# Order of the high and low weight products inside a weight-stationary unit of a decoder layer

## The chip, the cores and the metric

The kernel runs on one core of one Trainium2 chip. The metric is the device time of one launch in microseconds (us). The median of three runs before the change is 1451.52 us (1451.15 to 1453.07).

## The reference

One decoder layer for 256 tokens of width 2048, all in float32. Cut to its large products:

```
h      = rmsnorm(x)
q_a,k_a,v_a,q_r,f_r,i_r,g_r,gate_a,gate_r = split(h @ w_in)       # 2048 -> 11264
o_a    = causal attention(q_a, k_a, v_a)                          # 8 heads of 128
o_r    = gated linear recurrence(q_r, f_r, i_r), normed, gated    # 8 heads of 128
y      = sigmoid(gate_a + b_a) * (o_a @ w_up_a) + sigmoid(gate_r + b_r) * (o_r @ w_up_r)
x      = x + y @ w_out
out    = x + relu(rmsnorm(x) @ w_mlp1)^2 @ w_mlp2                 # 2048 -> 8192 -> 2048
```

## The kernel before

Every float32 factor is cut into two float32r parts, a high one (the value rounded to float32r, made on ScalarE) and a low one (what is left, made on VectorE), and a product of two factors is the sum of three: high by high, high by low, low by high. Activations lie with the width on the partitions: a "cat" tile of 128 x 512 holds the high parts of 256 tokens in columns 0 to 255 and their low parts in columns 256 to 511. `xcat`, `x2cat`, `mcat`, `orc` and `oac` are such tiles; there are 16 for a width of 2048.

Weights come in units of 128 x 2048 (1 MB). `load` brings a unit into a tile `raw` by the SP queue, `cut` (L107 to L118) makes the tiles `hi` (L116, ScalarE) and `lo` (L117, VectorE) of it, and `unit` (L123) hands out one unit while it loads and cuts the one two places ahead. `raw`, `hi` and `lo` have three buffers each.

A **weight-stationary unit** is the function `ws` (L278): it makes 128 output columns for all 256 tokens from 16 pieces of `hi` and `lo`, each 128 x 128. For each piece TensorE loads the high piece as weights and streams the whole cat tile past it (512 columns, called a wide product here), and loads the low piece and streams the high half of the cat tile (256 columns, a narrow product). Both add into one PSUM bank `pw`: the wide one into all 512 columns, the narrow one into columns 256 to 511. `summed` (L296) then copies the second half out on ScalarE (L298, `cross`) and adds the first half on VectorE (L299). The order before is: wide 0, narrow 0, narrow 1, wide 1, narrow 2, wide 2, and so on to narrow 15, wide 15 (L282 to L287). So each unit holds one place where a wide product follows a wide one (its first, behind the last of the unit ahead), one where a narrow product follows a narrow one, and otherwise alternates.

There are 152 units of 16 pieces: 72 for projections (`project`, on `xcat`), 16 for `w_out` (on `mcat`) and 64 for `w_mlp1` (on `x2cat`). A unit of the up-projections is used in two halves of 8 pieces, one on `orc` and one on `oac`; there are 16 of each. The rest of TensorE's work is not touched: products with activations as weights (`pv` L266 to L268 at the start, `py` L653 to L655 for `w_mlp2`), which are all 512 columns wide, and the small products of the recurrence and the attention, which run as side work between the units (`step`).

The queue of each engine is put in order by a scheduler that models the engines; program order is only its input. Where a product waits for data that come late, it may put later products ahead.

Of the kernel before, what the change touches and what calls it, by code (L numbers as in the profile page):

```python
# [17 lines left out]
T = 256  # L18
# [12 lines left out]
def layer_kernel(ctx: ExitStack, tc: tile.TileContext, xT, vecs, wv, wm, wg, wu, wo, w1, w2, cf, cm, out):  # L31
    nc = tc.nc
# [21 lines left out]
    def bank(s, pool=pp):  # L54
        return pool.tile([P, 512], F32, tag="b", name=uid(s))
# [67 lines left out]
    def unit():  # L123
        u = done[0]
        done[0] += 1
        load(u + AHEAD)
        cut(u + AHEAD)
        return split.pop(u)
# [127 lines left out]
    for c in range(4):  # L256
        pst = [bank(f"pv{t}", pm) for t in range(2)]
# [20 lines left out]
    def ws(parts, pst=None):  # L278

        pst = pst if pst is not None else bank("pw", pm)  # L280
        n = len(parts)
        for i, (h, l, cat) in enumerate(parts):  # L282
            if i == 0:
                nc.tensor.matmul(pst, h, cat, start=True, stop=False)  # L284
            nc.tensor.matmul(pst[:, T:], l, cat[:, :T], start=False, stop=False)  # L285
            if i > 0:
                nc.tensor.matmul(pst, h, cat, start=False, stop=(i == n - 1))  # L287
        return pst

    def unit_parts(hi, lo, cats, off=0):  # L290
        return [
            (hi[:, off + k * P : off + (k + 1) * P], lo[:, off + k * P : off + (k + 1) * P], c)
            for k, c in enumerate(cats)
        ]
# [8 lines left out]
    def project(dst):  # L303
        pst = ws(unit_parts(*unit(), xcats))
        s = s1("s")
        summed(pst, s)
        nc.vector.tensor_mul(dst, s, rstd)
# [258 lines left out]
    for j in range(KD):  # L566
        gr = s1("gr")
        project(gr)
        sig = nc.scalar.activation(gr, gr, AF.Sigmoid, bias=b_gate[:, 1, j : j + 1])
        with tc.issue_after(sig.ins):  # L570
            nc.scalar.activation(ga[j], ga[j], AF.Sigmoid, bias=b_gate[:, 0, j : j + 1])
        hi, lo = unit()
        pr = ws(unit_parts(hi, lo, orc, 1024))
        pa = ws(unit_parts(hi, lo, oac, 0))
        r = s1("r")
        summed(pr, r)
        nc.vector.tensor_mul(r, r, gr)
        a = s1("a")
        summed(pa, a)
        nc.vector.tensor_mul(a, a, ga[j])  # L580
        nc.vector.tensor_add(a, a, r)
        if j % 2 == 0:
            mt = g4("mcat", (P, 2, 512), F32R)
        to_parts((mt[:, j % 2, :T], mt[:, j % 2, T:]), a)
        mcat.append(mt[:, j % 2, :])
# [9 lines left out]
    for j in range(KD):  # L595
        pst = ws(unit_parts(*unit(), mcat))
# [30 lines left out]
    for part in range(4):  # L627
        ucat = []
        for j in range(16):
            pst = ws(unit_parts(*unit(), x2cats))  # L630
# [13 lines left out]
        for b in range(4):  # L644
            pst = [bank(f"py{t}", pm) for t in range(2)]
# [105 lines left out]
```

## Time and profile before

| what | us | share of the span |
|---|---|---|
| median of three runs | 1451.52 | |
| the profiled execution's own time | 1452.54 | |
| its span, first to last instruction | 1450.8 | 100% |
| TensorE matmuls busy | 1444.1 | 100% |
| TensorE weight loads busy | 1240.4 | 85% |
| VectorE busy | 894.3 | 62% |
| ScalarE busy | 690.6 | 48% |

Weight loads run beside matmuls, so the two do not add. The recorded end of a matmul is modelled and overlaps the next one's start; the distance from one start to the next is what a product takes in a row of products, and it is called a slot below. Starts are printed to 0.01 us, so a slot is best read over several products.

### The profile page before, as it was taken

Reading aid. Unit: us, or ns where it says so; the run is one execution under the profiler, and the core shown is the slowest. Engines: PE = TensorE matmul, PEld = TensorE weight load, DVE = VectorE, ACT = ScalarE, POOL = GpSimd, SP = SyncE. Lnnn points to the kernel's source line nnn. Section 1 sums busy time; section 2 is a strip of 40 time slices with the busy share of each in tenths; the row PEclk is TensorE's granted clock in tenths of the full one; section 3 lists DMA queues with packets and bytes.
Section 4 is the critical chain, followed back from the end, with each engine's and each line's share of the span. In section 5 each row is a group of like instructions: output and inputs, shape, how many; then the busy total and the mean of one; then the engine's idle time right before and its main releaser. Section 6 shows DMA issues by size and latency. Waiting matters only on the chain.

```text
span 1450.8 us, 18651 instructions
## 1 busy us (share of the span) xinstructions
PE 1444.1 (100%) x7824; PEld 1240.4 (85%) x7824; DVE 894.3 (62%) x958; ACT 690.6 (48%) x786; POOL 4.4 (0%) x10
## 2 busy tenths in 40 slices
PE   9999999999999999999999999999999999999998
PEld 7888889888888888888888888888888888888887
DVE  7545776667877667676666644565455655556553
ACT  7444343565765454544455443454335443355431
POOL 0000000000000000000000000000000000000000
PEclk9999999999999999999999999999999999999999
DMA  9555443445454465555545565556555566655571
GB/s 333 204 183 194 149 167 121 150 170 177 172 175 150 171 214 192 208 199 189 189 175 197 180 201 188 191 177 200 187 192 196 180 190 188 202 179 193 183 224 63
DMA packets 66323, 268.07 MB, mean 185 GB/s; under 512 B 4768, under 2 KB 7072, under 8 KB 43456
## 3 DMA queue, kind: packets, MB, share of 16 engines
q1 hardware_dynamic: 64368, 263.70, 53.3%
q0 software_dynamic: 576, 2.10, 0.4%
q8 instruction: 61, 1.00, 0.3%
q10 hardware_dynamic: 1296, 1.09, 0.2%
q14 instruction: 22, 0.18, 0.0%
HBM read 264.78 MB, written 2.10 MB: 184 GB/s over the span
## 4 chain that ended last, share of the span: by engine, by line
PE 99%; DMA 0%; DVE 0%; ACT 0%; issue 0%; DVEq 0%
PE pw L287 40%; PE pw L285 22%; PE py L653 8%; PE py L654 8%; PE py L655 8%; PE pw L284 3%; PE pv L266 2%; PE pv L267 2%; PE pv L268 2%; PE pd L363 1%; PE pl L491 0%; DMA raw<-wv 0%; PE pt L622 0%; PE pd L341 0%; PE pd L371 0%; PE pb L435 0%
## 5 line engine op out<-in xcount | busy, mean ns | idle before, releaser
L117 DVE TENSOR_TENSOR lo<-raw,hi 128x2048 fp32r<-128x2048 f32 (+2 forms) x258 | 569.4, 2208 | 317.6 <-ACT hi L116 317.5
L116 ACT ACTIVATE hi<-raw 128x2048 fp32r<-128x2048 f32 (+2 forms) x258 | 475.4, 1844 | 282.8 <-PE py L655 197.1
L287 PE MATMUL pw<-xcat,hi 128*128 128x512 f32 x1080 | 383.5, 397 | 0.0
L287 PE MATMUL pw<-x2cat,hi 128*128 128x512 f32 x960 | 342.4, 399 | 0.0
L285 PE MATMUL pw<-xcat,lo 128*128 128x256 f32 x1152 | 311.3, 280 | 0.0
L285 PE MATMUL pw<-x2cat,lo 128*128 128x256 f32 x1024 | 277.2, 281 | 0.0
L298 ACT ACTIVATE cross<-pw 128x256 f32<-128x256 f32 x168 | 64.5, 384 | 422.9 <-PE pw L287 422.9
L287 PEld LDWEIGHTS pw<-xcat,hi 128*128 128x128 f32 x1080 | 202.8, 188 | 46.3
L285 PEld LDWEIGHTS pw<-xcat,lo 128*128 128x128 f32 x1152 | 217.5, 189 | 5.2
L287 PEld LDWEIGHTS pw<-x2cat,hi 128*128 128x128 f32 x960 | 180.4, 188 | 42.0
L653 PE MATMUL py<-hi,ucat 128*128 128x512 f32 x512 | 199.5, 390 | 0.0
L655 PE MATMUL py<-hi,ucat 128*128 128x512 f32 x512 | 199.2, 389 | 0.0
L654 PE MATMUL py<-lo,ucat 128*128 128x512 f32 x512 | 199.2, 389 | 0.0
L285 PEld LDWEIGHTS pw<-x2cat,lo 128*128 128x128 f32 x1024 | 193.5, 189 | 5.4
L655 PEld LDWEIGHTS py<-hi,ucat 128*128 128x128 f32 x512 | 96.1, 188 | 20.0
L654 PEld LDWEIGHTS py<-lo,ucat 128*128 128x128 f32 x512 | 96.1, 188 | 19.9
L653 PEld LDWEIGHTS py<-hi,ucat 128*128 128x128 f32 x512 | 96.1, 188 | 19.7
L287 PE MATMUL pw<-mcat,hi 128*128 128x512 f32 x240 | 85.6, 399 | 0.0
L299 DVE TENSOR_TENSOR s<-pw,cross 128x256 f32<-128x256 f32 x72 | 30.4, 422 | 76.7 <-ACT cross L298 76.7
L299 DVE TENSOR_TENSOR t<-pw,cross 128x256 f32<-128x256 f32 x64 | 27.2, 425 | 77.0 <-ACT cross L298 77.0
L285 PE MATMUL pw<-mcat,lo 128*128 128x256 f32 x256 | 69.3, 281 | 0.0
L287 PEld LDWEIGHTS pw<-mcat,hi 128*128 128x128 f32 x240 | 45.1, 188 | 10.5
(180 smaller groups left out, 1245.0 us busy)
## 6 DMA issues: line engine op xcount, KB each, us to landing
raw<-w SPq DMA_DIRECT2D x128, 1024.0 KB, 5.3
raw<-wm SPq DMA_DIRECT2D x56, 1024.0 KB, 4.8
raw<-wg SPq DMA_DIRECT2D x16, 1024.0 KB, 4.8
raw<-wu SPq DMA_DIRECT2D x16, 1024.0 KB, 4.9
raw<-wo SPq DMA_DIRECT2D x16, 1024.0 KB, 4.8
raw<-wv SPq DMA_DIRECT2D x10, 1024.0 KB, 4.9
raw<-wv SPq DMA_DIRECT2D x8, 512.0 KB, 6.7
raw<-wv SPq DMA_DIRECT2D x8, 256.0 KB, 5.5
```

Source lines behind the costliest of these rows:

```text
L116: nc.scalar.activation(hi[:, s], raw[:, s], AF.Copy)
L117: nc.vector.tensor_sub(lo[:, s], raw[:, s], hi[:, s].bitcast(F32))
L266: nc.tensor.matmul(pst[t], xh, hi[:, k, :], start=(kk == 0), stop=False)
L267: nc.tensor.matmul(pst[t], xh, lo[:, k, :], start=False, stop=False)
L284: nc.tensor.matmul(pst, h, cat, start=True, stop=False)
L285: nc.tensor.matmul(pst[:, T:], l, cat[:, :T], start=False, stop=False)
L287: nc.tensor.matmul(pst, h, cat, start=False, stop=(i == n - 1))
L298: nc.scalar.activation(c, pst[:, T:], AF.Copy)
L299: nc.vector.tensor_add(dst, pst[:, :T], c)
L653: nc.tensor.matmul(pst[t], uh, hi[:, k], start=(kk == 0), stop=False)
L654: nc.tensor.matmul(pst[t], uh, lo[:, k], start=False, stop=False)
L655: nc.tensor.matmul(pst[t], ul, hi[:, k], start=False, stop=(kk == 15))
```

## The change

`ws` issues all wide products of a unit first, then all narrow ones. The group's start flag stays on the first product and the stop flag moves to the last narrow one. Nothing is added or removed.

```diff
         for i, (h, l, cat) in enumerate(parts):
-            if i == 0:
-                nc.tensor.matmul(pst, h, cat, start=True, stop=False)
-            nc.tensor.matmul(pst[:, T:], l, cat[:, :T], start=False, stop=False)
-            if i > 0:
-                nc.tensor.matmul(pst, h, cat, start=False, stop=(i == n - 1))
+            nc.tensor.matmul(pst, h, cat, start=(i == 0), stop=False)
+        for i, (h, l, cat) in enumerate(parts):
+            nc.tensor.matmul(pst[:, T:], l, cat[:, :T], start=False, stop=(i == n - 1))
```

TensorE in a unit of `w_mlp1`, before. A row is line, operation, output bank and its inputs, columns; "128x512" is a wide product, "128x256" a narrow one.

```order
L284 MATMUL pw_9980<-x2cat,hi_9914 128x512
L285 MATMUL pw_9980<-x2cat,lo_9915 128x256 x2
L287 MATMUL pw_9980<-x2cat,hi_9914 128x512
L285 MATMUL pw_9980<-x2cat,lo_9915 128x256
L287 MATMUL pw_9980<-x2cat,hi_9914 128x512
```

The same unit and the next one after the change (lines are two lower behind the changed function, and L283 and L285 are its wide and its narrow product):

```order
L283 MATMUL pw_9980<-x2cat,hi_9914 128x512 x16
L285 MATMUL pw_9980<-x2cat,lo_9915 128x256 x16
L283 MATMUL pw_10029<-x2cat,hi_9944 128x512 x16
L285 MATMUL pw_10029<-x2cat,lo_9945 128x256 x16
```

The alternation has become two runs of 16. The same holds for all units but a few at the borders of stages.

TensorE at one such border, the first unit of `w_out` after the change, whose last piece needs the `mcat` tile that is made last (`mcat_5302`; `pw_5421` is this unit's bank, `pw_5465` that of the next unit):

```order
L283 MATMUL pw_5421<-mcat_5302,hi_5308 128x512
L283 MATMUL pw_5465<-mcat_3895,hi_5354 128x512 x2
L283 MATMUL pw_5465<-mcat_4096,hi_5354 128x512 x2
L283 MATMUL pw_5465<-mcat_4297,hi_5354 128x512 x2
L283 MATMUL pw_5465<-mcat_4498,hi_5354 128x512 x2
L283 MATMUL pw_5465<-mcat_4699,hi_5354 128x512 x2
L283 MATMUL pw_5421<-mcat_5302,hi_5308 128x512
```

The first of these rows is the fifteenth wide product of the unit and the last row its sixteenth; the scheduler has put ten wide products of the next unit between them. The first unit of `w_mlp1` has the same with four products of the next unit. Before the change both units were in one piece.

ScalarE at the border of up-projection and `w_out`, before (`pw_5375` is the bank of the last half unit on `oac`; `hi_5417` is the cut two units ahead):

```order
L298 ACTIVATE cross_5393<-pw_5358 128x256
L298 ACTIVATE cross_5398<-pw_5375 128x256
L116 ACTIVATE hi_5417<-raw_5415 128x2048
L311 ACTIVATE mcat_5302<-a_5397 128x256
L116 ACTIVATE hi_5461<-raw_5459 128x2048
```

And after the change:

```order
L116 ACTIVATE hi_5417<-raw_5415 128x2048
L296 ACTIVATE cross_5398<-pw_5375 128x256
L309 ACTIVATE mcat_5302<-a_5397 128x256
L116 ACTIVATE hi_5461<-raw_5459 128x2048
L116 ACTIVATE hi_5507<-raw_5505 128x2048
```

The cut of the high part has moved ahead of the copy that takes the finished bank out of PSUM; the buffer that it fills is now read for the last time by the sixteenth wide product, halfway through the unit's 32.

## Rows read from the trace of the kernel before

**Rows 1.** The page's busy times (share of the span) and instructions of each engine.

```profile
PE 1444.1 (100%) x7824; PEld 1240.4 (85%) x7824; DVE 894.3 (62%) x958; ACT 690.6 (48%) x786; POOL 4.4 (0%) x10
```

**Rows 2.** The page's chain that ended last: share of the span by engine.

```profile
PE 99%; DMA 0%; DVE 0%; ACT 0%; issue 0%; DVEq 0%
```

**Rows 3.** The page's granted clock of TensorE in 40 slices, tenths of full speed.

```profile
PEclk9999999999999999999999999999999999999999
```

**Rows 4.** TensorE's two waits: who waited for whom, us, times, longest.

```profile
PE pwarm L159 <- DVE warm L156: 1.5, 1, 1.5
PE pv L266 <- ACT xcat L195: 1.2, 1, 1.2
```

**Rows 5.** Timeline of TensorE, one unit of `w_mlp1`: start us, us, engine, line, operation.

```profile
800.76 0.39 PE L284 MATMUL pw<-x2cat,hi 128*128 128x512 f32 x1
800.99 0.40 PE L285 MATMUL pw<-x2cat,lo 128*128 128x256 f32 x2
801.22 0.40 PE L287 MATMUL pw<-x2cat,hi 128*128 128x512 f32 x1
801.45 0.28 PE L285 MATMUL pw<-x2cat,lo 128*128 128x256 f32 x1
801.57 0.40 PE L287 MATMUL pw<-x2cat,hi 128*128 128x512 f32 x1
801.81 0.28 PE L285 MATMUL pw<-x2cat,lo 128*128 128x256 f32 x1
...
806.17 0.40 PE L287 MATMUL pw<-x2cat,hi 128*128 128x512 f32 x1
806.41 0.39 PE L284 MATMUL pw<-x2cat,hi 128*128 128x512 f32 x1
806.63 0.40 PE L285 MATMUL pw<-x2cat,lo 128*128 128x256 f32 x2
806.87 0.40 PE L287 MATMUL pw<-x2cat,hi 128*128 128x512 f32 x1
807.10 0.28 PE L285 MATMUL pw<-x2cat,lo 128*128 128x256 f32 x1
```

**Rows 6.** Timeline of TensorE in the `w_mlp2` stage, wide products alone.

```profile
860.07 0.39 PE L653 MATMUL py<-hi,ucat 128*128 128x512 f32 x1
...
865.51 0.39 PE L653 MATMUL py<-hi,ucat 128*128 128x512 f32 x1
```

**Rows 7.** Timeline of TensorE, two half units of the up-projection and the unit behind.

```profile
546.70 0.39 PE L284 MATMUL pw<-orc,hi 128*128 128x512 f32 x1
546.93 0.40 PE L285 MATMUL pw<-orc,lo 128*128 128x256 f32 x2
...
547.39 0.28 PE L285 MATMUL pw<-orc,lo 128*128 128x256 f32 x1
...
549.51 0.40 PE L284 MATMUL pw<-oac,hi 128*128 128x512 f32 x1
549.75 0.39 PE L285 MATMUL pw<-oac,lo 128*128 128x256 f32 x2
...
550.21 0.28 PE L285 MATMUL pw<-oac,lo 128*128 128x256 f32 x1
...
552.29 0.39 PE L284 MATMUL pw<-xcat,hi 128*128 128x512 f32 x1
```

**Rows 8.** Timeline of TensorE's weight loads behind a level of the recurrence.

```profile
167.22 0.19 PEld L284 LDWEIGHTS pw<-xcat,hi 128*128 128x128 f32 x1
167.33 0.42 PEld L285 LDWEIGHTS pw<-xcat,lo 128*128 128x128 f32 x2
```

**Rows 9.** Timeline of TensorE at the same place, matmuls.

```profile
167.25 0.48 PE L284 MATMUL pw<-xcat,hi 128*128 128x512 f32 x1
167.56 0.40 PE L285 MATMUL pw<-xcat,lo 128*128 128x256 f32 x2
```

**Rows 10.** Timeline of TensorE: first product of `w_out`, first of `w_mlp1`.

```profile
642.21 0.39 PE L284 MATMUL pw<-mcat,hi 128*128 128x512 f32 x1
...
732.56 0.39 PE L284 MATMUL pw<-x2cat,hi 128*128 128x512 f32 x1
```

**Rows 11.** Timeline of VectorE at these two places: a cut, last `mcat`, last `x2cat`.

```profile
644.70 2.29 DVE L117 TENSOR_TENSOR lo<-raw,hi 128x2048 fp32r<-128x2048 f32 x1 [0.46 <-ACT hi L116]
646.90 0.42 DVE L312 TENSOR_TENSOR mcat<-a,mcat 128x256 fp32r<-128x256 f32 x1
...
736.97 0.48 DVE L601 SCALAR_TENSOR_TENSOR x2cat<-x,vt,x2cat 128x256 fp32r<-128x256 f32 x1
```

## The prediction, made before the run

> **What bounds the kernel now.** I read the page's busy times first: TensorE's matmuls cover the whole span, VectorE has 62% and ScalarE 48% [rows 1]. The chain of work that ended last is TensorE for 99% [rows 2], the clock is granted in full in every slice, that is 2.4 GHz [rows 3], and TensorE waited for others only 1.5 + 1.2 us, both at the start [rows 4]. So the time is the sum of TensorE's slots, and the question is whether a slot depends on what stands beside it. A busy share cannot say that, because records of matmuls overlap; the starts in the timeline can.
>
> I then read one unit start by start [rows 5]. From the unit's first product to the next unit's first is 806.41 - 800.76 = 5.65 us; over the 16 units of `w_out` it is (732.56 - 642.21) / 16 = 5.647 us [rows 10]. From wide 1 to wide 15 there are 14 pairs in 806.17 - 801.22 = 4.95 us: **0.3536 us for a pair**. Where wide products stand alone, as in the `w_mlp2` stage, 24 of them take 865.51 - 860.07 = 5.44 us: **0.2267 us for a wide slot** [rows 6]. The wide product that opens a unit, behind another wide one, shows the same 0.23 us (800.76 to 800.99). If a wide slot in a pair is also 0.2267, the narrow one has 0.3536 - 0.2267 = **0.127 us**. A narrow product streams half the columns, and half of 0.2267 is 0.1133. So each lone narrow slot is 0.0136 us longer than its columns explain, 14 times in each of the 152 units and 6 times in each half unit, about 2300 times.
>
> **What the 0.0136 us is.** My reading is the weight load. The load for a product can only run while the product ahead streams, and a wide one gives it 0.2267 us, a narrow one half. How long such a load takes is seen where it has little cover: behind the short products of the recurrence the load for wide 0 is issued at 167.22 and narrow 0 starts at 167.56 [rows 8, 9]; the wide product between them takes its 0.2267, so it truly began at 167.333, which is 0.113 us after its load was issued, though it is recorded at 167.25. The next load follows 0.11 us behind [rows 8]. So a load takes about what a narrow product's columns take, and any delay in it lengthens the narrow slot. That is a tie, and the change decides how often it is fought: as often as before. Every product still has its own load, and every load behind a narrow product is still covered by 0.1133 us of columns alone. What changes is what stands around it.
>
> The term that decides is therefore the narrow slot in a run of narrow ones, which the trace shows only in twos: narrow 0 and narrow 1 of every unit. Taking the wide 1 behind them at 0.2267 and reading on to narrow 2, the two slots take 801.45 - 800.99 - 0.2267 = 0.233 us, in the next unit 807.10 - 806.63 - 0.2267 = 0.243 [rows 5], and in the half units 547.39 - 546.93 - 0.2267 and 550.21 - 549.75 - 0.2267 = 0.233 each [rows 7]. The mean is 0.236, that is 0.118 us for a narrow slot in a row of two. **Bounds:** not under 0.1133 (its columns), and on the other side the 0.127 of a lone one. I take 0.120, nearest to the twos, a little above them because a run of 16 gives no wide product in between to catch up.
>
> **The change part by part.** A whole unit becomes 16 x 0.2267 + 16 x 0.120 = 5.547 us instead of 5.647: 0.100 us less, 152 times, **15.2 us**. The two half units took 552.29 - 546.70 = 5.59 us [rows 7] (the one on `oac` is already quicker, 2.78 against 2.81) and become 5.547: 0.043 us, 16 times, **0.7 us**. Wide after wide costs 0.2267 as in `w_mlp2`. The number of products, columns and loads is the same, and the `py`, `pv` and side products keep their places.
>
> *At borders* the wide products come sooner and ask sooner for their cat tiles. The last `mcat` is finished at 646.90 + 0.42 = 647.32, which is 5.11 us after the first product of `w_out` [rows 10, 11]; wide 15 stood at 5.4 us and would now stand at 15 x 0.2267 = 3.4 us. Left so, it would stall 1.7 us. The scheduler fills this with ten wide products of the next unit, which puts it at 25 x 0.2267 = 5.67 us. For `x2cat` the tile is ready 736.97 + 0.48 - 732.56 = 4.89 us in, and wide 15 stands at 19 x 0.2267 = 4.31 us: a stall of 0.6 us, unless the chain to it is quicker than before, which it may be, because its high cut can now run before the last bank is finished. The last `mcat` has a high cut put ahead of it on ScalarE and a low cut of 2.29 us on VectorE [rows 11]; if the whole cut came on top, it would be late by 5.11 + 2.29 - 5.67 = 1.7 us. So the two borders cost between 0 and 2.3 us; I take **0.5 us**.
>
> *The buffers*: the high part's buffer is free halfway through its unit instead of at its end, so its cut on ScalarE may run earlier; the low part's buffer is free at the unit's end as before, its cut takes 2.29 us and is needed more than a unit later. The low cut stands ahead of some sums on VectorE's queue; behind these wait the copies of finished banks, of which there are four, so TensorE does not wait. ScalarE and VectorE stay at 48% and 62% of a span that is about 1% shorter.
>
> **Sum:** 15.2 + 0.7 - 0.5 = 15.4 us less. The profiled execution (1452.54 us, span 1450.8) would become 1437.1 us; it lies 1.0 us above the median of the runs, so the median goes from 1451.52 to **1436.1 us**.
>
> **A rule that speaks against it.** The Trainium skill, "TensorE: Matmul & The Clock Gate", section "Back-to-back issue gap", gives a warm product N / 2.4 ns + 2.5 ns, and section "LDWEIGHTS" gives a load of 128 columns 107 ns. By both, a slot depends on the product's own columns alone and the load just fits under 256 of them, so an estimate by that page leaves the sum of a unit at any order the same, and the change at nothing. The trace differs in that a wide product takes 227 ns and not 216, and a pair 354 and not 325. The second rival below is this rule's outcome.
>
> **The rivals.** *(1) A run of narrow products runs at its columns' pace.* Then loads overlap fully and the 0.0136 us belongs to changing from one width to the other. A unit becomes 16 x 0.340 + 0.0136 = 5.454 us, 0.193 less, and the half units 2 x (8 x 0.340 + 0.0136) = 5.467, 0.12 less: 152 x 0.193 + 16 x 0.12 - 0.5 = 30.8 us, **1420.7 us**. For it: the record of narrow 1 starts only 0.11 us behind narrow 0 where single starts can be told apart. Against it: the twos take 0.236 and not 0.2267 us.
>
> *(2) The narrow slot keeps its 0.127 us whatever stands beside it.* A unit is then 16 x 0.2267 + 16 x 0.127 = 5.659, 0.012 us more, the half units 0.069 more: 1.8 + 1.1 + 0.5 = 3.4 us more as a ceiling, **1451.5 to 1454.9 us**. For it: 14 pairs of each unit fit 0.2267 + 0.127 exactly, and the load argument makes no difference between the product behind. Against it: again the twos.
>
> *(3) Slower: weight loads behind one another fall behind.* A lone narrow slot is not even: in rows 5 narrow 2 to narrow 3 is 801.81 - 801.45 = 0.36 us, which leaves 0.133 for the narrow one. If without a wide product to catch up every load took that long, a unit would be 16 x 0.2267 + 16 x 0.133 = 5.755, 0.108 us more, and the half units 0.165 more: 16.4 + 2.6 + 0.5 = 19.5 us, **1471 us**. The point from which it is slower than a measurement can tell apart (0.2%, 2.9 us, used for the chances below) is a narrow slot near 0.1267 us.
>
> **How the numbers follow.** Forecast (narrow slot 0.117 to 0.123 us) 0.55; rival 1 0.17; rival 2 0.18; rival 3 0.10. The forecast alone spans 1428 to 1444 us. The range 1420 to 1455 takes in rivals 1 and 2 and both borders' bounds and leaves out rival 3 and little else. Faster by over 0.2% needs a narrow slot under about 0.125 us: the forecast, rival 1 and a small part of rival 2, 0.74. Within 0.2%: most of rival 2, 0.14. Slower: rival 3 and the upper edge of rival 2, 0.12.
>
> **What would show it.** In the timeline after, 16 wide starts 0.227 us apart and 16 narrow ones whose spacing is the number in question; a unit of 5.55 us; TensorE's waits still under 3 us in all plus some tenths at the starts of `w_out` and `w_mlp1`. Wide slots other than 0.227 us, a narrow slot outside 0.117 to 0.123 us, a wait of TensorE at each unit, or a lower clock would prove me wrong.

## The result and the profile after

The changed kernel took **1443.32 us** (median of four runs, 1441.81 to 1443.69) against 1451.48 us before: 0.994 of the time, 95% interval 0.9922 to 0.9957. Timed once more on another occasion it took 1441.74 us against 1452.89, 0.9928 (0.9915 to 0.994). It is faster, by 8 to 11 us; the forecast was 15.4 us less, the range 1420 to 1455.

The page after: the shares of the engines are those of [rows 1] within one point, the chain is TensorE for 99% as in [rows 2], the clock is granted in full as in [rows 3].

```profile
span 1441.9 us, 18721 instructions
...
PE 1435.0 (100%) x7824; PEld 1244.3 (86%) x7824; DVE 881.5 (61%) x958; ACT 695.2 (48%) x786; POOL 4.4 (0%) x10
```

TensorE's list of waits after, which answers [rows 4], has again the two of the start and no other:

```profile
PE pwarm L159 <- DVE warm L156: 1.5, 1, 1.5
PE pv L266 <- ACT xcat L195: 1.4, 1, 1.4
```

So TensorE's slots are still the time. Its timeline merges neighbours of one line, so a run of 16 is one row, and the distance from one row's start to the next is the run's length. One unit of `w_out` in the middle of its stage, and the first unit of the second `w_mlp1` pass, which follows 512-column products:

```profile
717.63 3.82 PE L283 MATMUL pw<-mcat,hi 128*128 128x512 f32 x16
721.28 2.08 PE L285 MATMUL pw<-mcat,lo 128*128 128x256 f32 x16
723.20 3.82 PE L283 MATMUL pw<-mcat,hi 128*128 128x512 f32 x16
...
905.38 3.79 PE L283 MATMUL pw<-x2cat,hi 128*128 128x512 f32 x16
909.00 2.08 PE L285 MATMUL pw<-x2cat,lo 128*128 128x256 f32 x16
910.92 1.32 PE L283 MATMUL pw<-x2cat,hi 128*128 128x512 f32 x5
```

The unit that follows wide products takes 910.92 - 905.38 = 5.54 us, 1.92 of it for 16 narrow products: 0.120 us each, the forecast's number. The unit that follows another unit takes 723.20 - 717.63 = 5.57 us: its narrow run is as long, but its wide run takes 3.65 instead of 3.62 us (the first five wide products behind a narrow run are longer by 0.027 us in sum). The forecast had 5.547 for all; before it was 5.647.

By stages, from the starts of the first products:

| stage | before, us | after, us | change | forecast |
|---|---|---|---|---|
| up to the first projection | 96.00 | 96.75 | +0.75 | 0 |
| 56 projections with the side work between | 368.31 | 365.93 | -2.38 | -5.6 |
| 16 projections and 16 pairs of half units | 177.90 | 176.89 | -1.01 | -2.3 |
| `w_out`, 16 units | 90.35 | 89.19 | -1.16 | -1.6, and a part of the border's +0.5 |
| `w_mlp1`, first pass | 90.79 | 89.55 | -1.24 | -1.6, and the rest of it |
| `w_mlp1`, the three others together | 271.04 | 267.12 | -3.92 | -4.8 |

The products of `w_mlp2` keep their order (87.04 and 87.07 us for a pass; the 0.03 us more are their first five products, which now stand behind a narrow run). The first line is not the change's: it ends before the first changed product, and in the second profile of the same kernel it was 94.61 us instead of 96.75. From there to the end the kernel before takes 1450.8 - 96.0 = 1354.8 us, the changed one 1441.9 - 96.75 = 1345.1 in one profile and 1439.8 - 94.61 = 1345.2 in the other. **The change itself is worth 9.6 us**; what else the medians differ by is the start.

Three of the rows behind this table, the first products of the projections, of `w_mlp1` and of `w_mlp2` after:

```profile
96.75 3.79 PE L283 MATMUL pw<-xcat,hi 128*128 128x512 f32 x16
...
728.76 0.63 PE L283 MATMUL pw<-x2cat,hi 128*128 128x512 f32 x2
...
818.31 0.40 PE L651 MATMUL py<-hi,ucat 128*128 128x512 f32 x1
```

### The profile page after: what moved, and what is told of

It is laid out like the page before. It is cut to its first block, busy times and chain, and to the rows that moved or that the text cites. A ratio compares the mean times of both kernels' runs of the same rounds, so it can differ in the third digit from the quotient of the medians.

```text
span 1441.9 us, 18721 instructions
## 1 busy us (share of the span) xinstructions
PE 1435.0 (100%) x7824; PEld 1244.3 (86%) x7824; DVE 881.5 (61%) x958; ACT 695.2 (48%) x786; POOL 4.4 (0%) x10
## 4 chain that ended last, share of the span: by engine, by line
PE 99%; DMA 0%; DVE 0%; ACT 0%; issue 0%; DVEq 0%
PE pw L283 43%; PE pw L285 22%; PE py L651 8%; PE py L653 8%; PE py L652 8%; PE pv L266 2%; PE pv L267 2%; PE pv L268 2%; PE pd L361 1%; PE pl L489 0%; DMA vt<-vecs 0%; PE pt L620 0%; PE pd L339 0%; PE pd L369 0%; PE pb L433 0%; PE pb L434 0%
## 5 line engine op out<-in xcount | busy, mean ns | idle before, releaser
L283 PE MATMUL pw<-xcat,hi 128*128 128x512 f32 x1152 | 278.0, 393 | 0.0
L283 PEld LDWEIGHTS pw<-xcat,hi 128*128 128x128 f32 x1152 | 212.0, 188 | 42.1
L283 PE MATMUL pw<-x2cat,hi 128*128 128x512 f32 x1024 | 244.4, 391 | 0.0
L283 PEld LDWEIGHTS pw<-x2cat,hi 128*128 128x128 f32 x1024 | 188.4, 188 | 36.8 <-DVE x2cat L599 0.2
L285 PEld LDWEIGHTS pw<-xcat,lo 128*128 128x128 f32 x1152 | 147.7, 191 | 5.6
L285 PE MATMUL pw<-xcat,lo 128*128 128x256 f32 x1152 | 149.4, 283 | 0.0
L285 PEld LDWEIGHTS pw<-x2cat,lo 128*128 128x128 f32 x1024 | 131.3, 191 | 4.9
L285 PE MATMUL pw<-x2cat,lo 128*128 128x256 f32 x1024 | 132.8, 283 | 0.0
L637 ACT ACTIVATE u<-t 128x256 f32<-128x256 f32 x64 | 26.4, 412 | 131.7 <-DVE t L635 131.7
L283 PE MATMUL pw<-mcat,hi 128*128 128x512 f32 x256 | 61.2, 391 | 0.0
L283 PEld LDWEIGHTS pw<-mcat,hi 128*128 128x128 f32 x256 | 47.0, 188 | 9.3 <-DVE mcat L310 0.3
L266 PE MATMUL pv<-hi,xcat 128*128 128x512 f32 x128 | 50.3, 400 | 1.4 <-ACT xcat L195 1.4
L267 PE MATMUL pv<-lo,xcat 128*128 128x512 f32 x128 | 50.5, 395 | 0.0
```

What stands on the lines that cost most here:

```text
L266: nc.tensor.matmul(pst[t], xh, hi[:, k, :], start=(kk == 0), stop=False)
L267: nc.tensor.matmul(pst[t], xh, lo[:, k, :], start=False, stop=False)
L283: nc.tensor.matmul(pst, h, cat, start=(i == 0), stop=False)
L637: nc.scalar.activation(u2, t, AF.Square)
```

## The experiments

All but alternating_load, which keeps the order of before, are edits of the changed kernel. `w_mlp1` has four passes of 16 units each, so one kernel can carry four forms of a unit, each read in the middle of its pass or over the whole of it (the first pass as a whole holds the border too, about 0.03 us a unit). Of the kernels that ran once only the timeline is used. The theory with which I went in: a weight load takes about as long as a narrow product's columns, so narrow products run at the load's pace.

### run_lengths: shorter runs

```diff
-        for i, (h, l, cat) in enumerate(parts):
-            nc.tensor.matmul(pst, h, cat, start=(i == 0), stop=False)
-        for i, (h, l, cat) in enumerate(parts):
-            nc.tensor.matmul(pst[:, T:], l, cat[:, :T], start=False, stop=(i == n - 1))
+        for r in range(0, n, run):
+            group = list(enumerate(parts))[r : r + run]
+            for i, (h, l, cat) in group:
+                nc.tensor.matmul(pst, h, cat, start=(i == 0), stop=False)
+            for i, (h, l, cat) in group:
+                nc.tensor.matmul(pst[:, T:], l, cat[:, :T], start=False, stop=(i == n - 1))
```

> The changed kernel, but in the four passes of w_mlp1 (16 units each) the wide and narrow products go in runs of 8, 4, 2 and 1 instead of 16 (w w.. n n.. w w..). In the changed kernel a run of n narrow products costs, over its columns, 0.0067 us for each but the first, and the wide run behind it 0.027 us in all. Theory A (the 0.027 us is a debt of fixed size that every narrow run leaves and that the wide products behind it pay in full): units of 5.44 + k x (0.0067 x (n - 1) + 0.027): 5.59 us for runs of 8, 5.63 for 4, 5.71 for 2, 5.87 for 1. Theory B (the debt grows with the run up to 0.027 us, and what a wide product cannot pay is carried on, never more than about 0.0136 us being lost for each lone narrow product): 5.59 for 8, about 5.62 for 4, 5.65 at most for 2, 5.65 for 1 as in the kernel before.

Timeline of TensorE: the first and the last of seven successive runs of 8 wide products in the first pass, then the first product of passes 2 to 4 and the first behind each:

```profile
766.46 2.00 PE L285 MATMUL pw<-x2cat,hi 128*128 128x512 f32 x8
...
783.22 2.00 PE L285 MATMUL pw<-x2cat,hi 128*128 128x512 f32 x8
...
903.80 0.39 PE L285 MATMUL pw<-x2cat,hi 128*128 128x512 f32 x1
...
993.59 0.40 PE L653 MATMUL py<-hi,ucat 128*128 128x512 f32 x1
...
1080.67 0.39 PE L285 MATMUL pw<-x2cat,hi 128*128 128x512 f32 x1
...
1169.84 0.40 PE L653 MATMUL py<-hi,ucat 128*128 128x512 f32 x1
...
1256.89 0.39 PE L285 MATMUL pw<-x2cat,hi 128*128 128x512 f32 x1
...
1347.33 0.40 PE L653 MATMUL py<-hi,ucat 128*128 128x512 f32 x1
```

A unit takes (783.22 - 766.46) / 3 = 5.587 us in runs of 8, (993.59 - 903.80) / 16 = 5.61 in runs of 4, 5.573 in runs of 2 and 5.653 in runs of 1. Theory A asked for 5.71 and 5.87 at the short end and falls. Theory B's values hold (5.59, about 5.62, at most 5.65, and 5.65), but it gives no reason why runs of 2 are 0.08 us cheaper than runs of 1, nearly as good as runs of 16, and better than runs of 4. Over the bare slots, 16 x (0.2267 + 0.120) = 5.547 us, one change from narrow to wide costs 0.020 us in runs of 8, as in the changed kernel's runs of 16, 0.016 in runs of 4, 0.003 in runs of 2 and 0.0066 in runs of 1. So the price is not a fixed one for each change.

### narrow_load: other loads and columns of the narrow products

```diff
-            nc.tensor.matmul(pst[:, T:], l, cat[:, :T], start=False, stop=(i == n - 1))
+            nc.tensor.matmul(pst[:m, T : T + w], l[:, :m], cat[:, :w], start=False, stop=(i == n - 1))
```

> The changed kernel, with other narrow products in the four passes of w_mlp1 (the last narrow product of each unit is left as it was); it leaves part of the low products out. Pass 1: weights of 64 columns instead of 128 (half of the outputs), 256 columns streamed. Pass 2: 128 weight columns, 192 streamed. Pass 3: 128 weight columns, 128 streamed. Pass 4: 64 weight columns, 128 streamed. Theory L (the weight load of the next product sets the narrow slot): pass 1 0.1133 us and no debt in the wide run, unit 5.44 us; passes 2 and 3 stay at 0.112 to 0.120 us, units 5.5 to 5.57; pass 4 about 0.060, unit 4.6. Theory S (the slot is set by the columns streamed, the rest by changing between widths): pass 1 0.120 us and unit 5.57 as without the edit; pass 2 0.085 to 0.092, unit 5.05; passes 3 and 4 0.057 to 0.063, unit 4.6.

One narrow run and the wide run behind it, passes 1 to 4:

```profile
763.79 1.99 PE L287 MATMUL pw<-x2cat,lo 128*64 128x256 f32 x16
765.62 3.81 PE L283 MATMUL pw<-x2cat,hi 128*128 128x512 f32 x16
...
932.93 1.95 PE L287 MATMUL pw<-x2cat,lo 128*128 128x192 f32 x16
934.73 3.83 PE L283 MATMUL pw<-x2cat,hi 128*128 128x512 f32 x16
...
1101.88 1.96 PE L287 MATMUL pw<-x2cat,lo 128*128 128x128 f32 x16
1103.67 3.83 PE L283 MATMUL pw<-x2cat,hi 128*128 128x512 f32 x16
...
1273.23 1.23 PE L287 MATMUL pw<-x2cat,lo 128*64 128x128 f32 x16
1274.30 1.99 PE L283 MATMUL pw<-x2cat,hi 128*128 128x512 f32 x8
```

Passes 2 and 3 settle one thing: with a quarter fewer and with half the columns the run of 16 takes 934.73 - 932.93 = 1.80 us and 1103.67 - 1101.88 = 1.79 us, 0.112 us a product either way. **That is the pace of loads of 128 columns, and with 192 and 128 streamed columns it binds.** Theory S is out there. Pass 4, with half the load as well, goes to 1274.30 - 1273.23 = 1.07 us. In pass 1 (half the load, all columns) the run falls from 1.92 to 1.83 us, towards theory L's 0.1133 us a product; but the wide run behind it keeps its extra 0.027 us (it takes 3.65 us in this pass too), which theory L had vanish.

### alternating_load: the same in the order of before

```diff
-            nc.tensor.matmul(pst[:, T:], l, cat[:, :T], start=False, stop=False)
+            nc.tensor.matmul(pst[:ml, c], l[:, :ml], cat[:, :w], start=False, stop=False)
             if i > 0:
-                nc.tensor.matmul(pst, h, cat, start=False, stop=(i == n - 1))
+                nc.tensor.matmul(pst[:m, :], h[:, :m], cat, start=False, stop=(i == n - 1))
```

> The order of before (alternating), with other shapes in the four passes of w_mlp1 (first and last wide product of each unit as they were); it leaves parts of the products out. Pass 1: the wide products load 64 weight columns instead of 128. Pass 2: the narrow ones load 64. Pass 3: the narrow ones stream 320 columns instead of 256. Pass 4: they stream 192. Theory L (the 0.0136 us of a pair is the load of the wide product not fitting under the narrow one's columns): pass 1 0.340 us a pair, unit 5.44 to 5.46; pass 2 0.3536 unchanged, unit 5.65; pass 3 0.2267 + 0.1417 = 0.368, unit 5.89; pass 4 0.3536 unchanged, unit 5.65. Theory S (0.0136 us is paid for changing the width): passes 1 and 2 unit 5.65, pass 3 5.89 + 0.20 = 6.10, pass 4 0.2267 + 0.085 + 0.0136 a pair, unit 5.19.

Pass 1, two wide products twelve pairs apart; then pass 3, a pair with 320 columns in the narrow product, and the narrow product three pairs later:

```profile
761.41 0.39 PE L289 MATMUL pw<-x2cat,hi 128*64 128x512 f32 x1
...
765.49 0.39 PE L289 MATMUL pw<-x2cat,hi 128*64 128x512 f32 x1
...
1099.78 0.31 PE L287 MATMUL pw<-x2cat,lo 128*128 128x320 f32 x1
1099.93 0.40 PE L289 MATMUL pw<-x2cat,hi 128*128 128x512 f32 x1
...
1100.92 0.31 PE L287 MATMUL pw<-x2cat,lo 128*128 128x320 f32 x1
```

In pass 1 a pair takes (765.49 - 761.41) / 12 = 0.340 us, theory L's number, and a unit in the middle of the pass 5.47: with lighter loads for the wide products the pair's excess is gone. In pass 3 a pair takes (1100.92 - 1099.78) / 3 = 0.380 us, not the 0.368 that theory L allows, though the narrow product's columns cover any load. So the excess in this pass is not a load that fails to fit. Over their passes (from the first product to the first of `w_mlp2`, divided by 16) the units of passes 1 and 2 took 5.49 and 5.52 us (theory L: 5.45 and 5.65; S: 5.65 in both), those of pass 3 took 6.07 (L 5.89, S 6.10) and those of pass 4 5.50, where L had 5.65 and S 5.19. L meets pass 1 and S nearly meets pass 3; neither theory is right as a whole.

What fits all the slots so far that load 128 columns is another rule, R: **columns at 2.4 GHz, plus 13.3 ns for every product**. 512 columns make 213.3 + 13.3 = 226.7 ns, 256 make 120.0, 320 make 146.7 (with 6.7 more in a pair, as 256 columns had it). I had taken half of a wide slot, 113.3, for the narrow product's columns; that is wrong by half of the fixed part.

### slot_rule: the rule on other shapes

```diff
-            nc.tensor.matmul(pst, h, cat, start=(i == 0), stop=False)
+            nc.tensor.matmul(pst[:mw, :], h[:, :mw], cat, start=(i == 0), stop=False)
-            nc.tensor.matmul(pst[:, T:], l, cat[:, :T], start=False, stop=(i == n - 1))
+            nc.tensor.matmul(pst[:mn, c], l[:, :mn], cat[:, :w], start=False, stop=(i == n - 1))
```

> The changed kernel, runs of 16, with other shapes in the four passes of w_mlp1; it leaves parts of the products out. Pass 1: the wide products but the first load 64 weight columns instead of 128. Pass 2: the narrow products but the last stream 384 columns instead of 256. Pass 3: the wide ones but the first load 32 weight columns. Pass 4: the narrow ones but the last load 32. Theory R (new, from the three runs before: a slot is the columns streamed at 2.4 GHz plus 0.104 ns for each weight column of the load that runs beside it, 13.3 ns for 128 of them, and at least 0.112 us for a load of 128 columns): wide slots of 0.220 us in pass 1 and 0.2167 in pass 3, narrow slots of 0.173 in pass 2 and 0.110 in pass 4. Theory P (slots grow in proportion to the columns, 17/16 of them, and the load only adds where it does not fit, as the prediction had it): wide slots of 0.2267 in passes 1 and 3, narrow ones of 0.170 in pass 2 and 0.1133 in pass 4.

Pass 2, then pass 1:

```profile
933.27 2.90 PE L289 MATMUL pw<-x2cat,lo 128*128 128x384 f32 x16
936.02 3.80 PE L284 MATMUL pw<-x2cat,hi 128*128 128x512 f32 x16
939.65 2.90 PE L289 MATMUL pw<-x2cat,lo 128*128 128x384 f32 x16
...
761.12 3.84 PE L284 MATMUL pw<-x2cat,hi 128*128 128x512 f32 x16
764.81 2.08 PE L289 MATMUL pw<-x2cat,lo 128*128 128x256 f32 x16
```

Fifteen products of 384 columns and one of 256 take 936.02 - 933.27 = 2.75 us. By rule R they are 15 x 0.1733 + 0.120 = 2.72 us, by theory P 15 x 0.170 + 0.113 = 2.66; the 0.03 us over R now stands in the narrow run, and the wide run behind has 939.65 - 936.02 = 3.63 us, at most 0.01 of it extra. R holds for products with 128 weight columns. Its second half, 0.104 ns for each weight column, fails: wide products that load 64 weight columns take 764.81 - 761.12 = 3.69 us for 16, 0.230 each, *longer* than full ones, and not 0.220; with 32 (pass 3) they took 3.71 us, 0.232 each, where R had 0.2167 and P 0.2267. So fewer weight columns did not make a run of wide products quicker, though they did so for narrow ones in narrow_load (0.112 to about 0.06 us with 128 columns streamed) and for the pairs of alternating_load's pass 1. What a lighter load changes depends on what it runs beside, and the passes with 64 and 32 columns say little about the load's length. Narrow products with 32 weight columns took 0.118 us in pass 4, where R had 0.110 and P 0.1133.

### debt_place: whose the 0.027 us is

```diff
-            nc.tensor.matmul(pst, h, cat, start=(i == 0), stop=False)
+            nc.tensor.matmul(pst[:mw, :], h[:, :mw], cat, start=(i == 0), stop=False)
```

> The changed kernel, runs of 16, with edits around the change from narrow to wide in the four passes of w_mlp1; it changes parts of the products. The five wide products behind a narrow run are 0.027 us longer in sum than five others. Pass 1: the second and third wide product load 64 weight columns instead of 128. Pass 2: the second to sixth do. Pass 3: the last narrow product streams all 512 columns, so that no load of a wide product runs beside a narrow one. Pass 4: all wide and narrow products but the first wide and the last narrow load 64. Theory D (a backlog of weight loads, worked off where loads have time to spare): with lighter loads it is worked off in fewer products, so in pass 1 and 2 the excess over the slots' own lengths falls below 0.015 us, in pass 4 to a few ns; pass 3 keeps it, one product earlier. Theory E (a price of changing the width, whatever is loaded): 0.02 us and more in all four.

Pass 3, a narrow run with its widened last product, the wide run, and the next narrow run:

```profile
1101.08 2.19 PE L289 MATMUL pw<-x2cat,lo 128*128 128x256 f32 x16
1103.10 3.81 PE L284 MATMUL pw<-x2cat,hi 128*128 128x512 f32 x16
1106.75 0.52 PE L289 MATMUL pw<-x2cat,lo 128*128 128x256 f32 x3
```

The wide run takes 3.65 us and the narrow one 1103.10 - 1101.08 = 2.02, which is 15 x 0.120 + 0.2267 within 0.01: the extra is still there although no load of a high piece runs beside a narrow product any more. Both theories had expected that of pass 3, so it does not part them; it shows only that the price does not come from those loads. In the other passes the excess did not fall as theory D had it: pass 1 as a whole takes 89.54 us, as in the changed kernel (89.55), and the wide runs of passes 2 and 4 take 3.67 and 3.68 us, longer than 3.65. But lighter loads had not made wide runs quicker in slot_rule either, so this is weak against D.

The changed kernel's own trace speaks against a backlog: the loads behind a narrow run do not start late. In the run of `w_out` shown above, which starts at 717.63 us, the loads of wide 1 to 4 start at 717.63, 717.87, 718.10 and 718.33, each with the product ahead of it and so 0.23 us before its own product, though a load keeps up at 0.112. One of them:

```profile
717.87 0.19 PEld L283 LDWEIGHTS pw<-mcat,hi 128*128 128x128 f32 x1
```

Theory E as worded (a price of changing the width, whatever is loaded) does not stand either: the price is 0.003 us behind runs of 2 and 0.020 behind runs of 8, and in alternating_load's pass 1 it went away with lighter loads. What the price depends on is open.

### entry_order: other beginnings of an alternating unit

```diff
+        seq = spread(("ww" + "nw" * 14 + "nn", "wwnn" + "wn" * 14, "www" + "nw" * 13 + "nnn", "wnn" + "wn" * 13 + "ww")[part])
```

> Alternating orders that begin a unit differently, in the four passes of w_mlp1 (w wide, n narrow): wwnwnw..nwnn, wwnnwnwn..wn, wwwnwn..nwnnn, wnnwnwn..wnww. In the kernel before, a pair took 0.3533 us in most units but 0.3465 in the half units on oac, which follow other products. Theory F (the two are stable rhythms, and what stands ahead decides which is entered): at least one of the four passes falls into the shorter rhythm and takes 16 x 0.3465 = 5.55 us a unit, less than the changed kernel's 5.566. Rival (the long rhythm is entered from every such beginning): 5.63 to 5.66 us in all four.

Pass 3, the beginnings of three units (wide 0 to 2):

```profile
1098.60 0.87 PE L286 MATMUL pw<-x2cat,hi 128*128 128x512 f32 x3
...
1104.16 0.85 PE L286 MATMUL pw<-x2cat,hi 128*128 128x512 f32 x3
...
1109.79 0.87 PE L286 MATMUL pw<-x2cat,hi 128*128 128x512 f32 x3
```

Units of 1104.16 - 1098.60 = 5.56 and 1109.79 - 1104.16 = 5.63 us take turns through the whole pass. Both rhythms exist and what stands ahead decides, as theory F says, but no pass stays in the short one, which F expected; passes 1 and 2 took 5.65 us. (The fourth pass lacks its sixteenth narrow product through a slip in the list and is not used.)

### two_units: half as many changes of width

```diff
+    def two(cats):
+        ...
+        wide(p0, b0)
+        wide(p1, b1)
+        narrow(p0, b0)
+        load(u + AHEAD)
+        cut(u + AHEAD)
+        narrow(p1, b1)
+        return b0, b1
```

> The changed kernel with two units taken together: 32 wide products into two banks, then 32 narrow ones; the two half units of the up-projection likewise. Half as many changes from narrow to wide. Theory A and B alike: a run of 32 costs 0.027 - 0.0067 = 0.020 us less than two runs of 16, so 76 x 0.020 + 16 x 0.020 = 1.8 us less than the changed kernel, about 1441.5 us. Rival (the second unit's cut and the side work move, and TensorE comes to wait for ScalarE or VectorE): a wait of tenths of a us in many units, 1444 us or more, and the waits show in the list of TensorE's waits.

```profile
936.35 7.44 PE L301 MATMUL pw<-x2cat,hi 128*128 128x512 f32 x32
943.63 4.00 PE L305 MATMUL pw<-x2cat,lo 128*128 128x256 f32 x32
947.47 7.44 PE L301 MATMUL pw<-x2cat,hi 128*128 128x512 f32 x32
```

Two units take 947.47 - 936.35 = 11.12 us, 5.56 each, and a wide run of 32 has one extra of 0.027 us (7.28 instead of 7.253). The time is 1440.88 us (0.9917, interval 0.9904 to 0.9931), the expectation was 1441.5. In a pass of `w_mlp1` that holds nothing but units the gain shows without the rest: the third takes 1167.87 - 1078.99 = 88.88 us, against 1170.52 - 1081.48 = 89.04 in the changed kernel, 0.16 us for 8 changes fewer, 0.020 each. Side by side with the changed kernel on one chip:

> The changed kernel as it is, beside the next run on the same chip: 8 to 9 us under the kernel before, 0.994 of its time.

> Two units taken together, as in two_units, beside the changed kernel on the same chip. If half as many changes from narrow to wide are what it gains (0.020 us each, 76 + 16 of them), it is 1.8 us under the changed kernel; if its first run only happened on a quicker chip, the two are alike within 1 us.

1441.74 us for the changed kernel and 1440.02 (0.9914, 0.99 to 0.9927) for two units together: 1.7 us less, where 1.8 was expected. (The changed kernel had been expected 8 to 9 us under the kernel before; here it was 11.) The intervals overlap, so the timing alone does not prove it; the pass of 88.88 us does. It is the quickest version of this study that computes the whole layer.

## Why the prediction was right, and where its sizes were off

**That slots are all that counts** held: TensorE's waits are those of before, and the stages without side work give back what their slots give. The time fell into the stated range, but the change was worth 9.6 us and not 15.4.

**The narrow slot of 0.120 us** was right to the last digit, for a wrong reason, and so by luck: 0.118 was read from the twos and 0.002 added for a catching up of loads that the runs do not show. It is not a tie between a load and the columns, but 256 columns plus a fixed 13.3 ns, as the 320 and 384 columns show. With that, rival 1 (0.1133 us) was never possible, and rival 3 (loads falling behind one another) neither, since a load of 128 columns keeps up at 0.112 us. Rival 2 (0.127 us in any order) is refuted by the runs of 16. The lone narrow slot of 0.127 never was there: it came from taking the wide slot of a pair at 0.2267, and [rows 5] say otherwise from start to start, 801.45 to 801.57 = 0.12 us for a lone narrow product and 801.57 to 801.81 = 0.24 for the wide one behind it. The excess of a pair stands in its wide slot. The same holds for the 0.133 of rival 3, which is this 0.36 less 0.2267.

**The step that failed in size is the sum of a unit**: 16 wide slots were taken at 0.2267 us, and the first five behind a narrow run are longer by 0.027 us together. That is 5.57 instead of 5.55, 0.08 saved instead of 0.10, 3 us over 152 units. I had put a pair's whole excess into the narrow slot and none into the wide ones. Part of it is paid at the change from one width to the other, as rival 1 read it, but on top of a narrow slot of 0.120, and more behind a long run than in a pair.

**The half units** were to give 0.7 us and gave next to nothing: with 8 products in a run the same 0.020 us is paid twice as often. One of them takes 639.57 - 636.78 = 2.79 us, two 5.58 us, against 5.59 before [rows 7].

```profile
636.78 2.00 PE L283 MATMUL pw<-oac,hi 128*128 128x512 f32 x8
...
639.57 0.63 PE L283 MATMUL pw<-mcat,hi 128*128 128x512 f32 x2
```

**The units behind side work** were counted as saving 0.100 like the others, and many save less or nothing. The first product of a unit behind a level of the recurrence stood at 167.25 us [rows 9], and that of the next unit behind a level at:

```profile
174.59 0.47 PE L284 MATMUL pw<-xcat,hi 128*128 128x512 f32 x1
```

A later unit behind a level, and the first product of the unit that follows it, stood at:

```profile
203.05 0.50 PE L284 MATMUL pw<-xcat,hi 128*128 128x512 f32 x1
...
209.97 0.50 PE L284 MATMUL pw<-xcat,hi 128*128 128x512 f32 x1
```

The same units after:

```profile
167.04 3.92 PE L283 MATMUL pw<-xcat,hi 128*128 128x512 f32 x16
...
174.41 3.92 PE L283 MATMUL pw<-xcat,hi 128*128 128x512 f32 x16
...
202.92 3.92 PE L283 MATMUL pw<-xcat,hi 128*128 128x512 f32 x16
...
209.76 0.50 PE L283 MATMUL pw<-xcat,hi 128*128 128x512 f32 x1
```

The first unit and its level take 174.59 - 167.25 = 7.34 us before and 174.41 - 167.04 = 7.37 after, the later ones 209.97 - 203.05 = 6.92 before and 209.76 - 202.92 = 6.84 after. Before, the first of the two alternates in the short rhythm that [rows 7] show on `oac` (0.3465 us a pair), the later in the long rhythm of [rows 5] (0.3533), which I took for all. Of the first 46 projections, whose side work stands alike in both kernels, 24 follow side work. Nine of these were in the short rhythm and take 0.03 to 0.04 us more after the change, six save 0.06, and nine save 0.08 to 0.10. I saw in [rows 7] that the half unit on `oac` was quicker and did not ask which other units were. So the projections gave 2.4 us instead of 5.6: about 1.1 of the missing 3.2 are the longer wide slots (56 x 0.020), and the rest is mostly the units that were in the short rhythm already.

**The borders** cost less than the 0.5 us taken. The last `mcat` is ready at 5.66 us after the start of `w_out`, as late as its product stands; its load waited 0.28 us, that of `x2cat` 0.20. `w_out` takes 89.19 us, 0.12 over 16 units of 5.567, and the first pass of `w_mlp1` gains 0.07 less than each of the others (1.24 against 1.31):

```profile
645.28 0.19 PEld L283 LDWEIGHTS pw<-mcat,hi 128*128 128x128 f32 x1 [0.28 <-DVE mcat L310]
...
733.04 0.19 PEld L283 LDWEIGHTS pw<-x2cat,hi 128*128 128x128 f32 x1 [0.20 <-DVE x2cat L599]
```

**The page's rule** of the Trainium skill ("TensorE: Matmul & The Clock Gate", "Back-to-back issue gap": columns / 2.4 ns + 2.5 ns, given there for a single product's gap) has the right form, a fixed part beside the columns; here the fixed part measures 13.3 ns with float32r operands and a load for every product. That order costs nothing, which would follow from it, is refuted by 5.653 us in runs of 1 against 5.565 in runs of 16.

**What stays open**: why a change from narrow to wide costs 0.020 us behind runs of 8 and more, 0.016 behind 4, 0.003 behind 2 and 0.0066 behind 1, and what the two rhythms of an alternating unit are. The runs show that the price of a long run does not come from the high pieces' loads beside narrow products, that lighter loads can take it away when widths alternate, and that the rhythm depends on what stands ahead; the mechanism is not shown.

## What to carry to other kernels

Where TensorE is the bound, read slots from start to start over many products, in several widths, before splitting a slot into parts: two widths already give the fixed part and the rate, and a guess of proportion hides it. Products of different width are best issued in runs, but the gain does not simply grow with the run: here a unit took 5.653 us in runs of 1, 5.573 in runs of 2, 5.61 in runs of 4, 5.587 in runs of 8, 5.565 in runs of 16 and 5.56 in runs of 32. Part of the gain can already be in place where other products break the alternation, so look at units behind each kind of neighbour, not at one unit. At 192 streamed columns and at 128, a product with its own 128-column float32r weights gains nothing from streaming less.

## What the hardware showed that was not expected

A slot of a float32r product with its own 128 x 128 load is its columns at 2.4 GHz plus 13.3 ns (226.7, 173.3, 146.7 and 120.0 ns for 512, 384, 320 and 256 columns) and not less than 112 ns. A run of wide products with weights of 64 columns is slower than with 128 (0.230 against 0.2267 us each). An alternating sequence has two rhythms, 0.3465 and 0.3533 us a pair, and can swap between them from unit to unit. The excess of a pair stands in its wide slot (0.24 us), not in the narrow one (0.12).
